# A written order for the first two recurrence blocks and their weights

## The chip, the cores and the metric

The kernel runs on one core of a Trainium2 chip. The metric is the device time of one launch in microseconds (us). TensorE (PE) multiplies matrices, VectorE (DVE), ScalarE (ACT) and GpSimd (POOL) do elementwise work, and SyncE (SP) only issues transfers; a transfer is run by 16 DMA engines. Each engine takes its instructions in the order in which its queue holds them, and waits where an operand is not there yet.

## The reference

One decoder layer on 2048 tokens of width 1024 in float32. The first half is normalised by its root mean square, projected, and given to two groups of heads that work side by side: a state-space mixer (SSD) with a short convolution, and an RWKV-7 recurrence. Their outputs are joined, projected and added; the second half is a gated feed-forward network with a convolution of three taps. The part that this change touches is the recurrence and the projection in front of it:

```python
def step(S, inp):
    r_t, w_t, k_t, v_t, a_t, b_t = inp
    sa = jnp.einsum("bhij,bhj->bhi", S, a_t)
    S = S * w_t[:, :, None, :] + sa[..., None] * b_t[:, :, None, :] + v_t[..., None] * k_t[:, :, None, :]
    return S, jnp.einsum("bhij,bhj->bhi", S, r_t)
```

Before it, each projected column is mixed with the one of the token before (`p + (shift(p) - p) * mu`), the decay `w` comes from a small network through tanh, keys are normalised per head, and the convolution of the SSD group (four taps) works on other projected columns.

## The kernel before

The recurrence phase (`phase_R`, L640) works on blocks of 128 tokens, 16 of them. It does not step through tokens: within a block the recurrence becomes products of 64-token halves, and a triangular system that is solved by substitution. Each float32 projection is made of float16 products: rows and weights are split into a high and a low part, and three of the four products are summed.

A `Block` (L730) is a set of named lists of small steps, and each step issues one or two instructions:

- `load` (L772): rows from memory, norm, split, and two transposes by DMA (L811 high part, L804 low part) into `xt`.
- `d(g)`, g from 0 to 13 (L816): one group of 128 projected columns, 24 products `d<-xt,wr`. For the odd g follow, for a pair of groups, in block 0 a copy `raw` out of PSUM (L835), the own part on ACT (L838) and the token shift on DVE (L841); results are `WA`, `GL`, `tk`, `tr`, `tv`.
- `low` (L903) gives `WX`, `zw`, `za` (the small network for decay and gate), `scan` (L944) sums the decays to `Pi` and `Pv`, `keys` (L960) and `norm` (L967) make normalised keys, with `nq` as the only product (L973), `receptance` (L999) gives `AR`.
- `gram` (L1011): products `gr<-AR,BK` and masks to `G` on DVE (L1024).
- `solve` (L1030): `G` goes to memory (`ATd`, L1038) and back in another layout (`atl`, L1041), `xl` is a constant (L1048). Then `chain`: 31 pairs of a product (L1059) and an addition (L1065), each pair depending on the one before, all on DVE. The result goes through memory to `XT`.
- `conv(g)`, g from 0 to 7 (L849): 24 products `c<-xt,wc`, `rc` on ACT (L863), taps on POOL and DVE (L881, L887), tanh on ACT (L893), a join on DVE (L898) and a store.
- `transposed`, `values`, `own`, `turn`, `merge`, `update`, `state`, `gate`, `finish`: the second half of the recurrence. `own`, `update` and `gate` read the state by products `pq` and `zg`, and `state` makes the new one (`pS`).

The weights come in 22 loads of 512 KB (`load_w`, L705): 14 for the projection (`wr`) and 8 for the convolution (`wc`). Each load lands in a staging tile `wst`, of which the even and the odd ones have two buffers each from load 2 on, and is split by ACT (high part, L598) and DVE (low part, L599). A call of `pace` keeps loads 4 and up behind block 0's transposes in SP's queue.

What sets the order: for block 0 the list `FIRST` is written for DVE and ACT, the other engines follow the scheduler. For block 1 (`SECOND`) the scheduler orders all engines. From block 2 on all engines but PE follow the list `PLAN`, whose steps are single ones. PE's order is the scheduler's throughout this phase.

Of the kernel before, what the change touches and what calls it, by code (L numbers as in the profile page):

```python
# [228 lines left out]
FIRST = """  # L229
w.0 w.1 l. w.2 w.3 w.4 w.5 f.d.0 f.d.1 f.low.0 f.d.2 f.d.3 f.d.4 w.6 f.low.1 w.7 f.d.5 f.scan w.8 f.keys w.9 w.10  # L230
f.norm f.d.6 f.d.7 w.11 w.12 f.d.8 f.d.9 f.receptance w.13 f.gram.0 w.14 f.d.10 w.15 f.gram.1 w.16 w.17 w.18 w.19
f.solve.1 f.chain.0 f.d.11 f.conv.0 f.chain.1 n.load f.conv.1.0 f.chain.2 f.taps.1 f.conv.2 f.d.12 f.chain.3 w.20
f.conv.3.0 f.transposed.0 w.21 f.conv.4 f.chain.4 f.chain.5 f.transposed.1 f.d.13 f.taps.3 f.conv.5.0 f.conv.6
f.chain.6 f.taps.5 f.chain.7 f.conv.7.0 f.taps.7
"""
# [404 lines left out]
def phase_R(tc, K, const, tables, x, w_r, w_c, wl_d, g2_d, XN, XC, YR, iters=16):  # L640
    nc = tc.nc
    V, S, G_ = nc.vector, nc.scalar, nc.gpsimd
    with ExitStack() as ctx:
# [86 lines left out]
        class Block(Steps):  # L730
# [1977 lines left out]
```

## Time and profile before

| what | value |
|---|---|
| median of the runs | 2508.16 us (2506.9 to 2513.34) |
| the profiled execution | 2506.49 us |
| its span | 2504.7 us |
| PE busy | 2396.9 us, 96% of the span |
| DVE / ACT / POOL busy | 1911.8 / 1197.9 / 1079.8 us |
| first product of PE | 15.5 us after the span's start |
| chain of block 0 begins | 68.6 us |
| chain of block 1 begins | 138.8 us |

How to read it: one execution is profiled, and its own time lies 1.8 us over its span. A row of the list in order of time has the start, the duration, the engine, the line, the operation with its output and inputs, and, in brackets, how long the engine had been idle and what released it. A `q` behind an engine (SPq) marks the issuing of a transfer. Where equal rows stand one behind another, one row covers several and gives their count.

### The profile page before, as it was taken

The numbers are of one execution on the slowest core, as the hardware profiler recorded it, in microseconds if no ns is written. First come the engines' busy times: TensorE is split into PE (matmuls) and PEld (weight loads), VectorE is DVE, ScalarE is ACT, GpSimd is POOL, SyncE is SP. The second block draws the span as 40 slices with busy tenths as digits, with TensorE's granted clock in tenths as the row PEclk, the third lists the DMA queues.
The fourth block names the chain that finished last, engine by engine and source line by source line (L and its number), as shares of the span: only waits on it lengthen the run. The fifth ranks groups of instructions, "written<-read, shape, count | busy, mean of one in ns | idle before, by whom it ended". The sixth has DMA issues, their size and how long they took to land. (4 is left out here: it accounts for less than half of the span.)

```text
span 2504.7 us, 53819 instructions
## 1 busy us (share of the span) xinstructions
PE 2396.9 (96%) x21212; PEld 1519.2 (61%) x21212; DVE 1911.8 (76%) x3790; ACT 1197.9 (48%) x2407; POOL 1079.8 (43%) x1134
## 2 busy tenths in 40 slices
PE   4899999999999999999988999999989999999998
PEld 4789999999999755555533444444434444444443
DVE  6767877787778667677999799999999735546557
ACT  6555666566656554445555544453543432213132
POOL 2243444344434532223335658685847522213135
PEclk8899999999999999999999999999999999999999
DMA  7233233323332536565774544444446533333243
GB/s 223 69 72 73 57 74 77 75 57 68 81 76 59 158 118 174 162 174 163 198 230 159 180 154 141 167 151 171 141 162 196 171 101 101 105 102 97 89 160 109
DMA packets 344412, 319.12 MB, mean 127 GB/s; under 512 B 203232, under 2 KB 248672, under 8 KB 340832
## 3 DMA queue, kind: packets, MB, share of 16 engines
q1 hardware_dynamic: 344016, 315.43, 43.1%
q8 instruction: 166, 2.72, 0.4%
q14 instruction: 86, 0.70, 0.1%
q10 hardware_dynamic: 144, 0.26, 0.0%
HBM read 187.85 MB, written 110.99 MB: 119 GB/s over the span
## 5 line engine op out<-in xcount | busy, mean ns | idle before, releaser
L2142 PE MATMUL u<-b,w 128*128 128x512 f16 x3696 | 808.5, 381 | 24.5 <-ACT C L2160 11.5
L2142 PEld LDWEIGHTS <-w 128*128 128x128 f16 x3696 | 362.8, 98 | 466.7 <-issue 35.6
L635 PE MATMUL d<-xt,wr 128*128 128x129 f16 x5376 | 335.6, 225 | 19.3 <-DMA xt<-xh 15.5
L635 PEld LDWEIGHTS <-wr 128*128 128x128 f16 x5376 | 322.0, 100 | 33.2 <-ACT wr L598 15.5
L2382 PE MATMUL d<-dw,fa 128*128 128x512 f16 x1512 | 333.6, 380 | 4.0 <-DMA dw<-DW 2.2
L2382 PEld LDWEIGHTS <-fa 128*128 128x128 f16 x1596 | 157.1, 98 | 204.7 <-issue 18.3
L2164 DVE TENSOR_TENSOR C<-u,C 128x512 f32<-128x512 f32 x220 | 150.5, 684 | 157.1 <-PE u L2142 151.4
L635 PE MATMUL c<-xt,wc 128*128 128x131 f16 x3072 | 197.9, 225 | 9.6 <-ACT rc L863 3.5
L635 PEld LDWEIGHTS <-wc 128*128 128x128 f16 x3072 | 183.8, 99 | 16.6 <-issue 9.3
L2395 DVE TENSOR_TENSOR acc<-d,acc 128x512 f32<-128x512 f32 x212 | 140.0, 682 | 54.3 <-PE d L2382 53.4
L1993 POOL TENSOR_TENSOR fa<-p,fa 128x512 f16<-128x512 f32 x100 | 140.7, 1421 | 50.7 <-ACT fa L1988 50.7
L2199 DVE SCALAR_TENSOR_TENSOR p<-C,fpar,p 128x1024 f32<-128x1024 f32 x88 | 124.3, 1412 | 34.5 <-ACT p L2195 34.4
L1995 DVE SCALAR_TENSOR_TENSOR w<-us,w 128x512 f16<-128x512 f32 x132 | 133.1, 1020 | 7.0 <-ACT w L1988 5.9
L887 DVE SCALAR_TENSOR_TENSOR ca<-c,cw,ca 128x128 f32<-128x128 f32 x360 | 113.5, 344 | 25.6 <-ACT ca L877 21.2
L1059 DVE TENSOR_TENSOR tmp<-atl,xl 128x60 f32<-128x60 f32 (+24 forms) x465 | 118.4, 255 | 16.4 <-DMA atl<-ATd 4.8
L2160 ACT ACTIVATE C<-u 128x512 f32<-128x512 f32 x88 | 52.2, 593 | 158.1 <-PE u L2142 134.4
L2199 DVE SCALAR_TENSOR_TENSOR a<-C,fpar,a 128x1024 f32<-128x1024 f32 x88 | 124.9, 1419 | 3.8 <-ACT a L2195 2.5
L1988 ACT ACTIVATE fa<-p 128x512 f16<-128x512 f32 x110 | 65.4, 623 | 124.6 <-DVE p L2212 112.7
L1065 DVE TENSOR_TENSOR xl<-xl,tmp 128x60 f32<-128x60 f32 (+24 forms) x465 | 112.5, 242 | 14.4
L1988 ACT ACTIVATE w<-us 128x512 f16<-128x512 f32 x132 | 80.2, 624 | 85.0 <-POOL us L2115 29.1
L2205 POOL COPY fcarry<-C 128x2 f32<-128x2 f32 x88 | 37.4, 426 | 161.2 <-DVE C L2164 161.2
L2115 POOL TENSOR_TENSOR us<-us,us 128x512 f32<-128x512 f32 x51 | 83.9, 1648 | 45.8 <-DVE w L1995 27.3
(334 smaller groups left out, 4308.1 us busy)
## 6 DMA issues: line engine op xcount, KB each, us to landing
UW<-w SPq DMA_DIRECT2D x154, 256.0 KB
w<-UW SPq DMA_DIRECT2D x154, 256.0 KB
us<-in_w_u_dram SPq DMA_DIRECT2D x88, 256.0 KB
DW<-dw SPq DMA_DIRECT2D x70, 256.0 KB
dw<-DW SPq DMA_DIRECT2D x56, 256.0 KB
hs<-HN SPq DMA_DIRECT2D x48, 256.0 KB
r<-in_w_d_dram SPq DMA_DIRECT2D x10, 1024.0 KB
xin<-in_x_dram SPq DMA_DIRECT2D x16, 512.0 KB
```

What stands on the lines that cost most here:

```text
L635: nc.tensor.matmul(ps, w[:, a, kt, :], xt[:, b, kt, cols], start=n == 0, stop=n == 3 * KT - 1)
L887: V.scalar_tensor_tensor(out=acc[:, q], in0=m["rc", e][:, q, k:k + 128], scalar=cw[:, e + q, k:k + 1], in1=acc[:, q], op0=ALU.mult, op1=AL ...
L1059: chain.tensor_tensor(out=self.tmp[:, :k, :n], in0=self.atl[:, j, j + 1:32].unsqueeze(1).to_broadcast([P, k, n]), in1=self.xl[:, :k, j:j + ...
L1065: chain.tensor_tensor(out=self.xl[:, :k, j + 1:32], in0=self.xl[:, :k, j + 1:32], in1=self.tmp[:, :k, :n], op=ALU.add)
L1988: S.activation(h, src, AF.Copy, **({} if scale is None else {"scale": scale}))
L1993: {"V": V, "G": G_}[engine].tensor_tensor(out=l, in0=src, in1=h, op=ALU.subtract)
L1995: V.scalar_tensor_tensor(out=l, in0=src, scalar=scale, in1=h, op0=ALU.mult, op1=ALU.subtract)
L2142: nc.tensor.matmul(bk[at], self.w[i][:, u, k, :], self.half.b[i][:, k, v, :], start=start and n == 0, stop=n == 11, skip_group_check=True)
L2164: op("V", .61, lambda: V.tensor_tensor(out=part(j, x), in0=bk[at], in1=part(*a), op=ALU.add), (("u", 4 * s + at), (*(c0, c1)[a[0]], a[1])) ...
L2199: V.scalar_tensor_tensor(out=o[j], in0=C[j][:, 2 - d:1026 - d], scalar=cw(g, 2 - d), in1=o[j], op0=ALU.mult, op1=ALU.add)
L2382: nc.tensor.matmul(bk[s, t], pairs[m].a[i][:, u, t * P:t * P + P], pairs[m].w[n][0][:, v, :], start=new and m == 0 and u == v == 0, stop=m ...
L2395: V.tensor_tensor(out=acc[j][:, t], in0=bk[s, t], in1=acc[j][:, t], op=ALU.add)
```

## The change

`FIRST`, `SECOND`, `load_w`, `load_wl`, the rule that paces the loads and the change of hands between blocks are replaced by one list, `HEAD`, of 665 single steps of blocks 0 and 1 and of the loads, followed by ACT, DVE, POOL and SP from the start. Loads and splits become steps too (`L.w.n/0` is the load n, the steps behind are its high and low parts, `L.low` is the two tiles of `wl`). PLAN is run from block 2. The instructions are the same, and so are the tiles and the arithmetic; only their order on the engines differs, up to the place where block 2 begins. The list ends with all of block 1's `solve`, so that the steps of it that PLAN's first round had issued are not issued again there.

```diff
-FIRST = """
-w.0 w.1 l. w.2 w.3 w.4 w.5 f.d.0 f.d.1 f.low.0 f.d.2 f.d.3 f.d.4 w.6 f.low.1 w.7 f.d.5 f.scan w.8 f.keys w.9 w.10
...
+HEAD = """
+L.w.0/0 L.low/3 R0.load/1 R0.load/2 L.w.0/5 R1.scan/2 R0.load/3 R0.load/0 L.w.1/0 L.w.2/0 R0.load/4 L.low/0 R0.load/5
...
-        def load_w(n):
...
-            d = nc.sync.dma_start(st, src[g:g + ng, :, k:k + nk, :].rearrange("g p k c -> p g k c"))
-            if n > 3:
-                pace(tc, K, d, "turned")
-            for i in range(nk):
-                split_w(tc, dst[:, g:g + ng, 0, k + i], dst[:, g:g + ng, 1, k + i], st[:, :, i], V, gwr[:, k + i:k + i + 1])
+        class Loads(Steps):
...
+            def w(self, n):
...
+                def rows():
+                    st = self.st[n] = wk.tile(
+                        [P, ng, nk, P], F32, name=f"wst{n}", tag="AR" if n < 2 else ("BT", "UV")[n % 2], bufs=2)
+                    nc.sync.dma_start(st, src[g:g + ng, :, k:k + nk, :].rearrange("g p k c -> p g k c"))
+
+                def hi(i):
+                    S.activation(dst[:, g:g + ng, 0, k + i], self.st[n][:, :, i], AF.Identity, scale=gwr[:, k + i:k + i + 1])
+
+                def lo(i):
+                    V.scalar_tensor_tensor(
+                        out=dst[:, g:g + ng, 1, k + i], in0=self.st[n][:, :, i], scalar=gwr[:, k + i:k + i + 1],
+                        in1=dst[:, g:g + ng, 0, k + i], op0=ALU.mult, op1=ALU.subtract)
+
+                return [rows, *(f for i in range(nk) for f in (lambda i=i: hi(i), lambda i=i: lo(i)))]
...
-        held = ExitStack()
-        held.enter_context(tc.manual_schedule(engines={getattr(mybir.EngineType, x) for x in ("DVE", "Activation")}))
-        for it in range(iters - 1):
...
+        loads = Loads()
+        K.hand.enter_context(tc.manual_schedule(engines=HANDS))
+        for step in HEAD.split():
...
+        for it in range(2, iters - 1):
+            for step in PLAN.split():
```

Below, names carry the block first (`tmp_0`, `tmp_1`), then a number of the buffer; lines of the changed kernel lie 54 to 81 higher than those of the old one.

At the start of the program, the queue of SP. Before:

```order
L663 DMA wls1_278<-in_wl_dram 128x512
L713 DMA wst2_282<-in_w_r_dram 128x4x256
L713 DMA wst3_288<-in_w_r_dram 128x4x256
L1048 DMA xl_0_800<-in_cst_dram 128x256
L811 DMA_TRANSPOSE xt_0_237<-xh_0_239 128x8x128
L804 DMA_TRANSPOSE xt_0_237<-xin_0_190 128x8x128
L713 DMA wst4_294<-in_w_r_dram 128x4x256
L713 DMA wst5_300<-in_w_r_dram 128x4x256
```

Now:

```order
L788 DMA wst2_263<-in_w_r_dram 128x4x256
L766 DMA wls0_265<-in_wl_dram 128x512
L788 DMA wst3_269<-in_w_r_dram 128x4x256
L788 DMA wst4_286<-in_w_r_dram 128x4x256
L788 DMA wst5_289<-in_w_r_dram 128x4x256
L892 DMA_TRANSPOSE xt_0_237<-xh_0_239 128x8x128
L885 DMA_TRANSPOSE xt_0_237<-xin_0_190 128x8x128
L788 DMA wst6_302<-in_w_r_dram 128x4x256
```

Loads 4 and 5 now stand ahead of the two transposes that the first product needs, and the load of `xl` stands later.

In the chain of block 0, the queue of DVE. Before, where the taps of the convolution (L887) and the splits of loads 20 and 21 (L599) stand in groups between pieces of the chain:

```order
L887 SCALAR_TENSOR_TENSOR ca_0_0_925<-rc_0_1_915,cw_216,ca_0_0_925 128x128 x6
L898 SCALAR_TENSOR_TENSOR ca_0_0_925<-ct_0_0_934,ca_0_0_925 128x256
L1059 TENSOR_TENSOR tmp_0_802<-atl_0_795,xl_0_800 128x4x19
L1065 TENSOR_TENSOR xl_0_800<-xl_0_800,tmp_0_802 128x4x19
L1059 TENSOR_TENSOR tmp_0_802<-atl_0_795,xl_0_800 128x4x18
```

Now:

```order
L1140 TENSOR_TENSOR tmp_0_981<-atl_0_888,xl_0_634 128x3x22
L794 SCALAR_TENSOR_TENSOR wc_203<-wst20_1022,gwr_235,wc_203 128x4x128
L1146 TENSOR_TENSOR xl_0_634<-xl_0_634,tmp_0_981 128x3x22
L1140 TENSOR_TENSOR tmp_0_981<-atl_0_888,xl_0_634 128x3x21
L794 SCALAR_TENSOR_TENSOR wc_203<-wst21_1045,gwr_235,wc_203 128x4x128
L1146 TENSOR_TENSOR xl_0_634<-xl_0_634,tmp_0_981 128x3x21
L1140 TENSOR_TENSOR tmp_0_981<-atl_0_888,xl_0_634 128x3x20
L968 SCALAR_TENSOR_TENSOR ca_0_0_976<-rc_0_1_968,cw_216,ca_0_0_976 128x128
```

Single splits and single taps stand between a product and its addition, or between two pairs.

At the start of block 2, the queue of DVE again. Before:

```order
L1059 TENSOR_TENSOR tmp_1_2093<-atl_1_2086,xl_1_2091 128x6x11
L841 SCALAR_TENSOR_TENSOR WA_2_2326<-d_2_0_2275,mus_204,WA_2_2326 128x128
L1065 TENSOR_TENSOR xl_1_2091<-xl_1_2091,tmp_1_2093 128x6x11
L841 SCALAR_TENSOR_TENSOR GL_2_2327<-d_2_0_2275,mus_204,GL_2_2327 128x128
L781 COPY xt_3_2397<-xt_2_2256 128x16x3
L1059 TENSOR_TENSOR tmp_1_2093<-atl_1_2086,xl_1_2091 128x6x10
L1065 TENSOR_TENSOR xl_1_2091<-xl_1_2091,tmp_1_2093 128x6x10
L914 TENSOR_TENSOR WX_2_2369<-WA_2_2326,WX_2_2369 64x128
```

Now:

```order
L1140 TENSOR_TENSOR tmp_1_2100<-atl_1_2022,xl_1_1953 128x8x2
L1314 TENSOR_TENSOR S0_0_227<-tS_01_2068,pS_01_2128 64x4x64
L1146 TENSOR_TENSOR xl_1_1953<-xl_1_1953,tmp_1_2100 128x8x2
L1140 TENSOR_TENSOR tmp_1_2100<-atl_1_2022,xl_1_1953 128x8
L1146 TENSOR_TENSOR xl_1_1953<-xl_1_1953,tmp_1_2100 128x8
L922 SCALAR_TENSOR_TENSOR WA_2_2323<-d_2_0_2272,mus_204,WA_2_2323 128x128
L922 SCALAR_TENSOR_TENSOR GL_2_2324<-d_2_0_2272,mus_204,GL_2_2324 128x128
L862 COPY xt_3_2394<-xt_2_1880 128x16x3
```

Block 2's token shift (`WA`, `GL`) was cut into the chain of block 1 two thirds of the way through, and now stands behind its last pair. PE's queue, which the scheduler sets, follows from this: `nq` of block 0 stood behind the fourth group of projections (d 4) and now stands behind d 6 and the first half of d 8; the products d 6 of block 1 now stand behind all of block 0's chain, since DVE's token shift of d 2 does.

More of the change, by code (lines that the diff above doesn't have):

```diff
@@ L228 @@
 )
-FIRST = """
-w.0 w.1 l. w.2 w.3 w.4 w.5 f.d.0 f.d.1 f.low.0 f.d.2 f.d.3 f.d.4 w.6 f.low.1 w.7 f.d.5 f.scan w.8 f.keys w.9 w.10
[L231 to L234, printed above, removed]
@@ new lines @@
+R0.receptance/3 L.w.16/1 R0.gram.0/2 R0.gram.1/2 L.w.17/1 R0.solve.1/1 R0.solve.1/0 L.w.17/3 L.w.16/3 R0.gram.1/1
+R0.d.11/1 R0.d.11/2 R1.load/5 L.w.17/4 R0.solve.1/3 L.w.16/4 L.w.18/1 R1.load/6 L.w.16/2 L.w.18/3 L.w.17/2
+R0.transposed.0/0 R0.d.12/0 R0.d.11/4 R0.solve.1/2 R0.conv.0/0 R0.d.11/3 L.w.19/1 R0.solve.1/4 L.w.19/2 L.w.18/4
+L.w.18/2 R0.conv.1.0/0 R0.conv.2/0 R0.conv.3.0/0 R1.load/7 R0.solve.1/6 R0.conv.1.0/1 R0.transposed.1/0 R0.solve.1/5
+R0.taps.1/0 L.w.19/3 R0.solve.1/7 L.w.19/4 R0.chain.0/0 R0.chain.0/1 R0.chain.0/2 R0.chain.0/3 R0.d.13/0 R0.chain.0/4
@@ new lines @@
+R1.d.5/1 R0.taps.7/6 R1.d.5/3 R0.taps.7/5 R1.d.5/2 R1.low.1/4 R0.taps.7/7 R1.low.1/2 R0.taps.7/8 R1.d.7/0 R1.low.1/3
+R1.d.5/4 R1.low.1/6 R1.keys/0 R1.d.8/0 R0.taps.5/0 R0.taps.7/9 R1.d.7/2 R2.load/1 R1.keys/1 R0.values/4 R0.chain.7/7
+R0.taps.5/1 R1.d.7/1 R1.norm/0 R1.d.7/3 R1.d.7/4 R0.taps.5/3 R0.taps.5/5 R1.norm/1 R0.taps.5/2 R0.chain.7/8 R1.scan/0
+R0.own.0/0 R1.d.9/0 R1.conv.0/0 R0.taps.5/4 R1.norm/4 R1.norm/2 R1.low.1/9 R1.scan/1 R1.d.9/1 R1.load/10 R1.low.1/7
+R0.taps.5/7 R1.low.0/6 R0.taps.7/10 R1.norm/5 R1.d.9/2 R1.norm/3 R1.conv.1/0 R0.taps.5/6 R1.d.9/3 R1.scan/3 R1.low.1/8
@@ new lines @@
+R0.taps.5/8 R1.d.9/4 R1.norm/9 R1.conv.1/1 R0.taps.5/9 R1.conv.2/0 R1.conv.1/2 R1.receptance/0 R1.conv.3/0 R0.own.0/1
+R1.conv.1/4 R1.conv.4/0 R1.conv.1/3 R1.norm/7 R1.conv.1/6 R1.norm/6 R0.chain.7/9 R1.scan/4 R0.chain.7/10 R0.chain.7/11
+R1.conv.1/5 R0.taps.5/10 R1.norm/10 R1.conv.1/7 R1.conv.1/8 R1.conv.1/9 R1.norm/8 R1.norm/11 R0.own.0/2 R0.turn/0
+R0.turn/1 R0.merge.0/0 R0.chain.7/12 R1.conv.1/10 R1.conv.3/1 R1.conv.3/3 R1.conv.3/2 R0.chain.7/13 R1.conv.3/5
+R1.norm/12 R0.merge.0/2 R1.conv.3/4 R0.merge.0/1 R1.gram.0/0 R1.gram.0/1 R1.conv.3/7 R1.gram.0/2 R2.load/2 R1.conv.3/6
@@ new lines @@
+R0.merge.1/0 R1.gram.1/0 R1.conv.5/0 R0.merge.1/1 R0.update.0/0 R1.conv.5/1 R1.gram.1/1 R1.gram.1/2 R1.conv.3/8
+R1.receptance/2 R2.load/0 R1.conv.3/9 R1.conv.6/0 R1.conv.3/10 R1.conv.1/11 R2.load/3 R1.receptance/4 R1.conv.5/2
+R1.solve/0 R1.conv.5/4 R0.update.0/1 R1.conv.5/3 R1.conv.5/5 R1.receptance/3 R1.solve/1 R1.conv.5/7 R1.solve/3
+R1.solve/2 R2.load/4 R1.conv.7/0 R1.conv.3/11 R1.solve/8 R2.load/5 R2.load/6 R0.state.0/2 R0.merge.1/2
+R1.transposed.0/0 R1.conv.7/1 R1.conv.5/6 R1.conv.5/8 R0.state.0/5 R0.own.1/0 R1.d.10/0 R1.solve/4 R0.state.0/3
@@ new lines @@
+R1.conv.7/2 R1.conv.7/4 R0.state.0/4 R1.conv.7/6 R1.receptance/1 R0.state.0/6 R1.conv.7/3 R1.solve/7 R0.own.1/1
+R2.load/7 R0.gate/0 R1.solve/5 R0.own.1/2 R0.update.1/0 R0.update.1/1 R0.state.1/5 R0.state.1/6 R0.finish.0/0
+R0.state.1/0 R0.state.1/1 R1.solve/6 R1.d.11/0 R1.conv.7/8 R1.conv.7/5 R1.conv.7/7 R1.d.11/1 R1.solve/9 R1.solve/10
+R1.solve/11 R1.conv.5/9 R1.solve/12 R1.solve/13 R1.solve/14 R1.solve/15 R1.solve/16 R1.solve/17 R1.solve/18
+R1.solve/19 R1.solve/20 R1.solve/21 R1.solve/22 R1.solve/23 R1.solve/24 R1.solve/25 R1.solve/26 R1.solve/27
@@ L241 @@
+R1.conv.5/11 R1.solve/55 R1.solve/56 R0.finish.0/4 R1.solve/57 R1.d.13/3 R1.solve/58 R1.solve/59 R1.solve/60
+R1.solve/61 R1.solve/62 R1.solve/63 R1.solve/64 R0.gate/1 R1.solve/65 R1.solve/66 R1.solve/67 R1.transposed.1/0
+R0.state.1/3 R1.solve/68 R1.solve/69 R1.solve/70 R1.solve/71 R1.solve/72 R1.solve/73 R1.conv.7/11 R1.solve/74
+R1.solve/75 R1.solve/78 R1.solve/76 R2.load/10 R1.transposed.1/1 R1.solve/77
 """
```

104 lines of the change are left out of this document (62 added, 42 removed).

## The prediction

> **What bounds the kernel now.** I read the page first, then a table of stretches over the first 200 us, then the waits of TensorE, then the order in time of the places where it waits. From the page:
>
> ```profile
> span 2504.7 us, 53819 instructions
> PE 2396.9 (96%) x21212; PEld 1519.2 (61%) x21212; DVE 1911.8 (76%) x3790; ACT 1197.9 (48%) x2407; POOL 1079.8 (43%) x1134
> PE   4899999999999999999988999999989999999998
> ```
>
> TensorE (PE) is busy for 96% of the span, and its first slices (62.6 us each) are the empty ones. The table of stretches has, for each, its length, then busy time of PE, weight loads, VectorE (DVE), ScalarE (ACT), GpSimd, then PE's granted clock, the DMA share and GB/s:
>
> ```profile
> 12.00:16.00 4.00, 0.27 (x1) 0.14 (x2) 3.94 (x8) 4.00 (x8) 0.00 (x0) 1.00 1.12 202
> 16.00:28.00 12.00, 11.79 (x159) 11.77 (x158) 8.28 (x17) 8.44 (x23) 0.14 (x1) 1.00 1.08 323
> 28.00:52.00 24.00, 9.92 (x107) 8.39 (x105) 17.14 (x27) 18.80 (x37) 9.43 (x10) 0.73 0.48 147
> 52.00:69.00 17.00, 12.95 (x150) 11.41 (x149) 13.01 (x22) 9.38 (x16) 2.68 (x3) 0.80 0.58 160
> 69.00:84.00 15.00, 9.38 (x75) 8.12 (x74) 13.59 (x46) 5.21 (x10) 4.09 (x5) 0.61 0.73 185
> 84.00:105.00 21.00, 20.94 (x318) 20.10 (x319) 15.27 (x63) 9.40 (x28) 2.46 (x5) 0.93 0.11 24
> 105.00:146.00 41.00, 37.05 (x637) 34.54 (x635) 26.79 (x82) 22.92 (x47) 13.20 (x15) 1.00 0.28 65
> 146.00:166.00 20.00, 17.78 (x270) 16.26 (x267) 15.68 (x53) 10.90 (x30) 8.27 (x8) 1.00 0.05 8
> 166.00:200.00 34.00, 34.00 (x605) 32.18 (x604) 24.89 (x82) 20.01 (x42) 13.09 (x16) 1.00 0.46 95
> ```
>
> From 166 us on PE is full; before that it idles: 15.5 us before its first product, 14.1 in 28 to 52, 4.1 in 52 to 69, 5.6 in 69 to 84, 4.0 in 105 to 146, 2.2 in 146 to 166, 46 with the crumbs. That is all this change can touch: the products stay the same, and from block 2 on each engine keeps its order. So I forecast when block 2's first projections end, and carry that shift to the end. Where the middle ones come from (engine, line, total, times, longest), for PE from 28 to 146 us:
>
> ```profile
> PE nq L973 <- ACT sq L964: 9.0, 1, 9.0
> PE gr L1019 <- DVE AR L1006: 5.1, 1, 5.1
> ```
>
> The key norm `nq` holds PE while its input is made elsewhere, and the gram waits for DVE.
>
> **The change part by part.** First the **start**. Rows are start, duration, engine, line, operation, and in brackets the idle time before and its releaser:
>
> ```profile
> 11.20 1.35 SPq L811 DMA_TRANSPOSE xt<-xh  x1
> 15.52 0.27 PE L635 MATMUL d<-xt,wr 128*128 128x129 f16 x1 [15.52 <-DMA xt<-xh]
> 21.50 0.39 ACT L835 ACTIVATE raw<-d 128x258 f32<-128x258 f32 x1
> ```
>
> The first product waits for the transpose, issued at 11.20 and done at 15.5. Now loads 4 and 5 (1.05 MB) stand ahead of it and the 0.13 MB load of `xl` does not: 0.92 MB more. At the 323 GB/s of 16 to 28 us that is 2.8 us, if the transposes wait for the bytes ahead; 0 if they overtake them. I take 2.8: the first product at 18.3, `raw` at 24.3. [...]
>
> **From `raw` to the chain of block 0.** First two stretches in the columns of the table above, from `raw` to the end of ACT's split of load 15 and (for the next part) from the chain of block 0 to block 1's d 6; then rows in order of time:
>
> ```profile
> 21.50:53.40 31.90, 17.82 (x226) 16.06 (x224) 22.80 (x41) 25.70 (x56) 9.57 (x10) 0.77 0.61 191
> 68.60:104.70 36.10, 30.25 (x391) 27.99 (x389) 29.22 (x108) 14.71 (x37) 6.25 (x10) 0.80 0.36 90
> ...
> 51.40 2.08 PE L1019 MATMUL gr<-AR,BK 64*128 64x128 f32 x16 [5.09 <-DVE AR L1006]
> 52.09 1.33 ACT L598 ACTIVATE wc<-wst,gwr 128x512 f16<-128x512 f32 x2 [1.94 <-DMA wst<-in_w_c_dram]
> 57.52 1.28 DVE L1024 TENSOR_TENSOR G<-gr,cst 128x512 f32<-128x512 f32 x2
> 58.83 0.82 SPq L1038 DMA_DIRECT2D ATd<-G  x2
> 64.42 1.71 SPq L1041 DMA_DIRECT2D atl<-ATd  x4
> 68.61 0.19 DVE L1059 TENSOR_TENSOR tmp<-atl,xl 128x31 f32<-128x31 f32 x1 [2.45 <-DMA atl<-ATd]
> ```
>
> ACT is busy for 25.70 of the 31.9 us; with the same steps packed it would be at that place at 24.3 + 25.7 = 50.0 instead of 52.09 + 1.33 = 53.4. `nq` now stands behind d 6, so PE does not wait 9.0 us for it, and the weights are split earlier. But the gram does not profit by 9: it waits for `AR` on DVE, which waits for ACT and GpSimd, and PE comes to it at 51.8 by the same walk (before 51.40). Its masks `G` end about 1 us earlier, at 57.9; with the 68.61 - 58.80 = 9.8 us that the round trip through DRAM takes, `atl` would be there at 67.7; the loads that it shared the queue with are further ahead, and DVE's own list (split of load 19) is done at 67.2. I take the latter: **-1.4** (bounds: -4.2 where the transposes overtake the loads, +1 where ACT loses 2.4 of its 3.4 again).
>
> **The chain of block 0.** The solve is 31 pairs of a product and an addition on DVE:
>
> ```profile
> L1059 DVE TENSOR_TENSOR tmp<-atl,xl 128x60 f32<-128x60 f32 (+24 forms) x465 | 118.4, 255 | 16.4 <-DMA atl<-ATd 4.8
> L1065 DVE TENSOR_TENSOR xl<-xl,tmp 128x60 f32<-128x60 f32 (+24 forms) x465 | 112.5, 242 | 14.4
> 76.65 1.66 DVE L887 SCALAR_TENSOR_TENSOR ca<-rc,cw,ca 128x128 f32<-128x128 f32 x6
> 78.79 0.42 DVE L898 SCALAR_TENSOR_TENSOR ca<-ct,ca 128x256 f32<-128x256 f32 x1 [0.48 <-ACT ct L893]
> 81.28 2.73 DVE L599 SCALAR_TENSOR_TENSOR wc<-wst,gwr,wc 128x512 f16<-128x512 f32 x4
> 103.26 5.68 PE L635 MATMUL d<-xt,wr 128*128 128x129 f16 x96
> ```
>
> The 31 pairs take 15.4. In the last row 24 products end d 4 of block 1, then d 6 begins: 103.26 + 24/96 x 5.68 = 104.7, 36.1 us after the chain began. In these DVE was busy for 29.22 us (the second stretch above) and idle for 6.9; PE was short of work in 69 to 84 and full in 84 to 105: it did late what waited for taps and splits behind pieces of the chain. The list now mixes single taps and splits into the chain, and d 6 of block 1 stands behind DVE's token shift of d 2, which stands just behind the chain's end. DVE has till there 31 x (0.255 + 0.242) = 15.4, twelve taps 12 x 0.277 = 3.3, four splits 2.7, two joins 0.8, and some 12 small steps that I price at 0.3 each, 3.7: 25.9 us if nothing makes it wait (3.3 of the 29.22 now stand before or after it). PE's own work from 60 us up to there, some 25.6 us of products, would end at 85.6, so DVE decides: d 6 at 67.2 + 25.9 = 93.1 instead of 104.7. That is **-10.2**, the largest term; its bounds are -19 (PE's floor) and -3.3 (DVE waits as long as before, 6.9).
>
> **From there to block 2.** This took from 104.7 to 145.7 (below), 37.05 of it busy, the same as in 105 to 146. The second half of `za` and the first reading of the state (`pq`) move into it:
>
> ```profile
> 100.29 1.15 PE L1179 MATMUL pq<-UV,G 64*64 64x64 f32 x32
> 102.36 0.39 PE L928 MATMUL zw<-WX,wl 128*128 128x128 f16 x4
> 102.81 0.39 PE L928 MATMUL za<-WX,wl 128*128 128x128 f16 x4
> ```
>
> `pq` takes 102.36 - 100.29 = 2.1, `za` 103.26 - 102.81 = 0.45: 39.6 of work. Of the 4.0 of stalls I keep 1.5 (the others end on DVE and ACT steps that the list puts earlier), and add 1.5 for some 15 hand-overs between engines at 0.1 that a walk by durations does not see: 42.6, **+1.6** (bounds -1.4 and +4).
>
> **Block 2's first projections.** The list finishes all of block 1's chain before DVE's token shift of block 2:
>
> ```profile
> 138.83 0.19 DVE L1059 TENSOR_TENSOR tmp<-atl,xl 128x31 f32<-128x31 f32 x1 [2.36 <-DMA atl<-ATd]
> 144.28 4.31 PE L635 MATMUL d<-xt,wr 128*128 128x129 f16 x72
> 151.96 0.34 DVE L841 SCALAR_TENSOR_TENSOR WA<-d,mus,WA 128x128 f32<-128x128 f32 x1
> 154.78 0.39 PE L928 MATMUL zw<-WX,wl 128*128 128x128 f16 x4
> 161.23 4.30 PE L635 MATMUL d<-xt,wr 128*128 128x129 f16 x72
> ```
>
> d 0 of block 2 began at 144.28 + 1.44 = 145.7; `WA` was cut into the chain at 151.96; `zw` needed it. Now the gram ends at 93.1 + 20.5 of products + 0.5, its masks at 115.3, the chain begins 9.8 later at 125 and takes 15.4 + 3.6 of other steps, so `WA` at 144 and `zw` at 145.8, 1.8 later. PE, with d 0 begun at 135.7, reaches `zw` 8.1 us later at 143.8 (before 154.78 - 145.7 = 9.1, about 1 of it waiting): a wait of 2.0 in place of the 2.2 there: **0**. Behind `WA` stand on DVE `GL`, the copy of `xt` and `WX`; ACT's tanh waits for it.
>
> **The clock.** It was 0.73 in 28 to 52 and 0.61 in 69 to 84, behind long waits. Fewer long waits mean less of that, but a walk at full speed between 42 and 70 us is too good: 0 to +2, I take **+1.0**. [...]
>
> **Sum:** -1.4 - 10.2 + 1.6 + 0 + 1.0 = -9.0 us. The profiled execution took 2506.49 (span 2504.7 and 1.8 around it), 1.7 below the median of 2508.16. I take the sum off the median: 2508.16 - 9.0 = 2499. With its bounds the forecast's own range is a gain of 3 to 15: 2493 to 2505.
>
> **Rivals.**
> **Larger gain:** the transposes overtake the loads, the chain starts at about 64, and DVE's small steps find free slots, so that PE is nearly at its floor: 2.8 + about 13, near 16 us, 2492. For it speaks that DVE was idle for 6.9 us there; against, that the chain's 15.4 us cannot shrink.
> **No change:** the start costs 2.8, ACT's packed walk slips by 3 (a step written in order makes all behind it wait), the pieces of the chain wait as before: -9.0 + 6 = a gain of about 3, 2505. For it speaks that ACT is busy for only 18.8 of 24 us in 28 to 52 although its order was written already.
> **Slower:** block 1's chain ahead of `WA`. If its `atl` arrives no earlier than in the trace (138.83), `WA` is at 157.8 and `zw` at 159.6 against 154.78: +4.8, and up to +8 with the clock halved after that wait, about 2514. It decides from a chain start of about 134 on. Against it: the gram in front stands earlier by 10 us.
> That the change does nothing is excluded: PE's queue differs from the first 48 products on.
>
> **How the numbers follow.** A measurement here tells about 0.3% from no change, 7.5 us. Forecast 0.55, of which 0.45 lies above 7.5 us; larger gain 0.20; no change 0.15; slower 0.10, of which 0.08 is beyond 7.5 us; what is left of each counts as no change. Faster 0.45 + 0.20 = 0.65, slower 0.08, the same 0.27. The range reaches from 2487 (larger gain with all bounds good: 21 us, the -19 with the better start) to 2508 (no gain): about 0.1 is left out above, less below.
>
> **What would show it.** In the changed kernel: the first product at 18.3 (15.5 if transposes overtake); no wait at `nq`; the chain of block 0 at 67.2 and d 6 of block 1 at 93.1 (the step most likely to fail); d 0 of block 2 at 135.7; a wait of about 2 at `zw`; from there the same products in the same time. I am wrong if DVE waits inside the first chain, or if d 6 comes after 100.

## The result, and the profile after

The changed kernel takes 2491.06 us (median of 5 runs, 2487.77 to 2499.62), the kernel before 2508.16 (median of 5 runs, 2505.32 to 2513.34). The ratio is 0.9934, with a 95% interval of 0.9912 to 0.9957: 17 us by the medians, 11 to 22 by the interval. The prediction was 2499 with a range of 2487 to 2508.

The profiled execution is the slowest of the five (2499.62). Its page:

```profile
span 2497.8 us, 53811 instructions
PE 2398.1 (96%) x21210; PEld 1519.3 (61%) x21212; DVE 1909.4 (76%) x3790; ACT 1197.4 (48%) x2407; POOL 1082.4 (43%) x1134
```

The busy times over the whole span are those of before. The table of stretches of the changed kernel, in the same cuts and columns as before:

```profile
16.00:28.00 12.00, 6.74 (x84) 6.30 (x85) 8.18 (x15) 6.81 (x16) 0.00 (x0) 1.00 0.90 249
28.00:52.00 24.00, 16.34 (x209) 15.08 (x206) 18.96 (x33) 22.31 (x49) 10.26 (x10) 0.79 0.55 178
52.00:69.00 17.00, 12.00 (x161) 11.34 (x160) 14.97 (x25) 9.20 (x17) 6.83 (x6) 0.89 0.77 193
69.00:84.00 15.00, 13.25 (x201) 12.53 (x198) 14.33 (x62) 6.24 (x16) 1.10 (x2) 1.00 0.20 49
84.00:105.00 21.00, 20.87 (x352) 19.87 (x350) 18.80 (x60) 14.62 (x34) 9.03 (x12) 1.00 0.37 91
105.00:146.00 41.00, 39.54 (x673) 37.15 (x672) 31.33 (x115) 22.03 (x53) 13.75 (x14) 1.00 0.28 54
146.00:166.00 20.00, 20.00 (x362) 18.41 (x361) 13.71 (x33) 14.52 (x30) 10.79 (x13) 1.00 0.34 85
```

In 16 to 28 us PE is worse off (6.74 busy instead of 11.79) and in 52 to 69 no better (12.00 instead of 12.95). In the others it is better off or as good: 16.34 instead of 9.92 in 28 to 52, 13.25 instead of 9.38 in 69 to 84, and full in 146 to 166, where it had lost 2.2. The waits of PE up to 170 us (total, times, longest; four of them) show that the long waits at `nq` and for `AR` are gone and shorter ones stand elsewhere instead:

```profile
PE d L689 <- ACT wr L791: 17.9, 1, 17.9
PE d L689 <- ACT tr L919: 4.8, 1, 4.8
PE c L689 <- ACT tv L919: 3.5, 1, 3.5
PE nq L1054 <- ACT sq L1045: 1.0, 1, 1.0
```

The places in time on which the prediction stood, in the changed kernel (start, duration, operation): the first product, the products with both parts of the rows, the first and the last pair of block 0's chain, d 6 of block 1, the first pair of block 1's chain, d 0 and `WA` of block 2, and the key norm `nq` of block 2.

```profile
17.91 0.27 PE L689 MATMUL d<-xt,wr 128*128 128x129 f16 x1 [17.91 <-ACT wr L791]
18.61 5.58 PE L689 MATMUL d<-xt,wr 128*128 128x129 f16 x70 [0.43 <-DMA xt<-xin]
68.25 0.18 DVE L1140 TENSOR_TENSOR tmp<-atl,xl 128x31 f32<-128x31 f32 x1
88.53 0.18 DVE L1140 TENSOR_TENSOR tmp<-atl,xl 128x8 f32<-128x8 f32 x1
90.30 1.55 PE L689 MATMUL d<-xt,wr 128*128 128x129 f16 x24
119.67 0.18 DVE L1140 TENSOR_TENSOR tmp<-atl,xl 128x31 f32<-128x31 f32 x1
131.27 2.93 PE L689 MATMUL d<-xt,wr 128*128 128x129 f16 x48
137.21 0.34 DVE L922 SCALAR_TENSOR_TENSOR WA<-d,mus,WA 128x128 f32<-128x128 f32 x1
148.33 1.12 PE L1054 MATMUL nq<-sq,cst 128*128 128x512 f32 x2
```

The last of these before:

```profile
165.37 1.08 PE L973 MATMUL nq<-sq,cst 128*128 128x512 f32 x2
```

So the key norm of block 2 comes 165.37 - 148.33 = 17.0 us earlier, the gain of the medians. The term that made most of it lies between the start of block 0's chain and d 6 of block 1: 90.30 - 68.25 = 22.05 us, before 36.1.

The 17.0 us can also be split by what PE did. The first 166 us, before and now:

```profile
0.00:166.00 166.00, 120.06 (x1702) 110.73 (x1702) 117.35 (x329) 96.12 (x203) 44.73 (x60) 0.90 0.45 124
0.00:166.00 166.00, 128.75 (x2020) 120.67 (x2022) 125.79 (x359) 105.91 (x226) 56.23 (x70) 0.96 0.49 132
```

PE idled 45.9 us before and idles 37.3 now, 8.7 less. The other 8.3 us are products that take less time: up to the key norm of block 2 PE is busy for 111.1 us now (128.75 less the full stretch from 148.33 to 166) and was busy for 119.4, with 1700 products in both traces. The granted clock is the third figure from the right: its mean over these 166 us is 0.96 instead of 0.90.

**One thing must be taken out of the profiled span.** It is only 2504.7 - 2497.8 = 6.9 us shorter. The other 10 us were lost after 800 us, where nothing was changed, at the passage from the recurrence to the next phase. There PE waits as long as before (3.1 us, before 3.2), and the granted clock falls earlier and for longer (its mean is 0.91 over the 130 us from 813 on, before 0.97 over the 130 us from 830 on). First the wait, the stretch behind it and a later stretch before, then the same of the changed kernel:

```profile
PE vt L1112 <- ACT tg L1255: 3.2, 1, 3.2
850.00:860.00 10.00, 9.94 (x136) 7.68 (x135) 5.91 (x14) 5.27 (x12) 8.07 (x20) 1.00 0.11 25
880.00:890.00 10.00, 9.37 (x102) 5.80 (x104) 4.80 (x7) 4.68 (x12) 1.15 (x2) 0.66 0.59 187
```

```profile
PE vt L1193 <- ACT tg L1336: 3.1, 1, 3.1
833.50:843.50 10.00, 10.00 (x104) 7.60 (x103) 3.03 (x9) 4.42 (x10) 6.97 (x19) 0.66 0.02 9
873.50:883.50 10.00, 10.00 (x62) 5.19 (x62) 4.64 (x8) 3.15 (x9) 2.68 (x3) 0.50 0.43 158
```

The granted clock stayed at 1.00 behind the wait before and fell to 0.66 here; later it fell in both, to 0.66 before and to 0.50 here. For that reason the experiments are read by the key norm of block 2 and not by one span.

### The profile page after: what moved, and what is told of

It is laid out like the page before. It is cut to its first block, busy times and chain, and to the rows that moved or that the text cites. A ratio compares the mean times of both kernels' runs of the same rounds, so it can differ in the third digit from the quotient of the medians.

```text
span 2497.8 us, 53811 instructions
## 1 busy us (share of the span) xinstructions
PE 2398.1 (96%) x21210; PEld 1519.3 (61%) x21212; DVE 1909.4 (76%) x3790; ACT 1197.4 (48%) x2407; POOL 1082.4 (43%) x1134
## 5 line engine op out<-in xcount | busy, mean ns | idle before, releaser
L2051 ACT ACTIVATE w<-us 128x512 f16<-128x512 f32 x132 | 80.3, 624 | 85.6 <-PE u L2205 28.6
```

The costliest lines, as they stand in the source:

```text
L2051: S.activation(h, src, AF.Copy, **({} if scale is None else {"scale": scale}))
```

## The experiments

All start from the changed kernel but one, which starts from the one before. Times in us; the third column is d 6 of block 1, the fourth the key norm of block 2; the rest is the span less the fourth.

| kernel | chain of block 0 | d 6 | key norm | span | rest |
|---|---|---|---|---|---|
| before | 68.6 | 104.7 | 165.4 | 2504.7 | 2339.3 |
| changed | 68.3 | 90.3 | 148.3 | 2497.8 | 2349.5 |
| changed, again | 66.8 | 88.8 | 146.9 | 2490.1 | 2343.2 |
| loads 4 and 5 swapped | 68.0 | 90.1 | 148.0 | 2497.2 | 2349.2 |
| load steps by the list | 65.7 | 87.7 | 145.7 | 2487.9 | 2342.2 |
| tv early | 66.8 | 89.2 | 147.3 | 2488.6 | 2341.3 |
| split early | 66.8 | 90.3 | 148.3 | 2491.1 | 2342.8 |
| chain in closed pieces | 68.4 | 96.2 | 154.2 | 2494.6 | 2340.4 |
| block 1's chain left to the steady list | 67.1 | 89.1 | 146.8 | 2490.1 | 2343.3 |
| first part written only | 68.4 | 91.0 | 156.6 | 2498.0 | 2341.4 |
| second part written only | 76.4 | 96.5 | 154.5 | 2495.1 | 2340.6 |
| before, key norm late | 70.7 | 107.4 | 168.0 | 2512.0 | 2344.0 |
| three edits together | 65.8 | 88.3 | 146.3 | 2489.3 | 2343.0 |
| and tr early | 67.1 | 91.0 | 150.3 | 2488.7 | 2338.4 |

**The changed kernel again**, no edit.

> The changed kernel once more, unchanged. Its first profile gained 17.0 us up to the key norm of block 2 (165.37 before, 148.33 after), but only 6.9 in the span, because TensorE's clock fell to 0.66 and 0.50 in two stretches of 10 us between 833 and 884 us behind a wait of 3.1 us, which in the kernel before (3.2 us) left the clock at 1.00. Theory A (the clock drop is a matter of one execution): the key norm of block 2 is at 148.3 +-0.3 again, and the span is either near 2488 without the drop or near 2498 with it. Theory B (the drop belongs to the changed kernel): the clock is below 0.7 at the same place again and the span is 2497 to 2499.

The key norm came at 146.85, outside the 0.3 that I had allowed, since the chain started 1.4 us earlier: the head differed by about 1.5 us between the two executions. The clock fell again (0.66 in 830 to 840, 0.78 and 0.70 in 860 to 880), but less, and the span is 2490.1. Neither theory holds as put: the drop is not always the same, and it is not a matter of one execution either. The rest differs from 2338 to 2350 between kernels that are the same there, and the span of one execution can't tell less than that.

**Transposes ahead of loads 4 and 5.**

```diff
- ... R0.load/8 R0.load/9 ... L.w.4/0 ... L.w.5/0 ...
+ ... R0.load/8 R0.load/9 L.w.5/0 L.w.4/0 ...
```

> Loads 4 and 5 are issued behind the two transposes instead of ahead of them, the rest of the list is unchanged. Theory A (the transposes wait for the bytes ahead of them, and the head up to the first chain is a chain of dependent steps): the first product moves from 17.9 to about 15.5 us, and block 0's solve (68.25) and the key norm of block 2 (148.3) come 2.4 us earlier. Theory B (the start is covered, because ACT and the later loads set the pace): the first product comes earlier, but block 0's solve and block 2's key norm move by less than 0.5 us. Theory C (the transposes overtake the loads): the first product stays at 17.9, which its row puts down to ACT's split.

This moved nothing but the order of loads 4 and 5 between themselves. The list names the transposes ahead of both loads already, but block 0's `load` is called in full before the list begins, so its places in the list are empty, and SP had both loads first. The run is one more execution of the changed kernel as far as the rest goes: 148.0.

**Block 0's load steps by the list.**

```diff
         blocks = [Block(it) for it in range(iters)]
-        blocks[0].do("load")
         loads = Loads()
```

> The earlier try to put the transposes ahead of loads 4 and 5 only swapped those two loads, because block 0's load steps are issued before the list begins, so their places in the list do nothing. Here that call in front is taken out, and the load steps follow the list: both transposes stand ahead of loads 4 and 5 in SP's queue, and ACT splits one piece of a weight before the norm. Theory A (bytes issued ahead delay the transposes): the transposes are issued at about 10.6 us as before, the first product comes at 15.5 to 16.5 instead of 17.9. What follows of it: if the head is one chain of dependent steps, the start of block 0's solve (68.25, 66.8 and 68.0 in three looks) and the key norm of block 2 (148.3, 146.9, 148.0) come 2 us earlier; if ACT and the later loads set the pace, both stay in 66.5 to 68.5 and 146.5 to 148.5; since loads 4 and 5 now wait for the transposes to be issued, they could even be 1 to 2 us later. Theory B (transposes overtake, ACT's split sets the start): the first product stays at 17.7 to 18.4.

From the list in order of time:

```profile
14.07 0.27 PE L689 MATMUL d<-xt,wr 128*128 128x129 f16 x1 [14.07 <-DMA xt<-xh]
14.92 5.18 PE L689 MATMUL d<-xt,wr 128*128 128x129 f16 x61 [0.58 <-DMA xt<-xin]
```

With both parts PE begins at 14.92 instead of 18.61: 3.7 us earlier, of which 0.5 is from an earlier issue of the transposes (10.12 instead of 10.61). From the issue of the first transpose to this product it takes 8.0 us in the changed kernel and in the run with loads 4 and 5 swapped, where the two loads stand ahead, and 4.8 here, where they do not. So here the transposes waited for the bytes ahead of them; the 2.8 us of the prediction were 3.2. But behind that the chain starts only 1.1 to 2.6 us earlier than in the three executions of the unchanged order, and so does all else: PE waits for ACT's own parts of `tr` (6.1 us) and `tk` (2.3) and for splits on DVE (2.4) in between. About half of what the start loses is covered later.

**One step of ACT earlier, two ways.** `tv` is what PE waits for before the first convolution product (3.5 us); the split is what DVE waits for ahead of the chain (1.9 us).

```diff
- R0.d.11/1 R0.d.11/2 R1.load/5 ... R1.load/6 ... R0.d.11/3 L.w.19/1
+ R0.d.11/1 R0.d.11/2 R0.d.11/3 R1.load/5 ... R1.load/6 ... L.w.19/1
```

> One ACT step is moved: the second half of the own part of group 11 (tv) directly behind its first half, ahead of block 1's norm, its float16 copy and two splits. In the changed kernel PE waits 3.46 us for it before the first convolution product (61.8). Theory P (in the chain's time PE is full from there to d 6 of block 1, so an earlier convolution carries through): the first convolution product moves 2.5 to 3 us ahead, d 6 of block 1 from 22.0 us to 20 us or less behind the chain's start or the chain starts earlier too, and the key norm of block 2 comes at 144.5 to 146. Theory D (DVE's list decides when d 6 starts): the convolution starts earlier, but d 6 and the key norm of block 2 stay (146.5 to 148.5), because the chain does not start earlier.

```diff
- R0.conv.1.0/1 ... L.w.19/3 R0.solve.1/7 L.w.19/4 R0.chain.0/0
+ L.w.19/3 R0.conv.1.0/1 ... R0.solve.1/7 L.w.19/4 R0.chain.0/0
```

> One ACT step is moved: the last high part of load 19 ahead of the copy of the first convolution group out of PSUM, for which ACT waited 4.0 us; DVE's low part of it stands directly ahead of the chain and waited 1.9 us. Theory D (DVE's list decides): the chain starts about 2 us earlier (at 65.5 to 66.5), and d 6 of block 1 and the key norm of block 2 come 2 us earlier (145 to 146.5). Theory P (PE is full): the chain starts earlier, d 6 comes no more than 0.5 us earlier, and the key norm of block 2 stays at 146.5 to 148.5.

With `tv` early (the first convolution products and the next ones):

```profile
57.38 0.98 PE L689 MATMUL c<-xt,wc 128*128 128x131 f16 x14
61.88 3.08 PE L689 MATMUL c<-xt,wc 128*128 128x131 f16 x34 [3.52 <-DVE wc L794]
```

The convolution begins 3.3 to 4.4 us earlier, and d 6 (89.2) and the key norm (147.3) lie where theory D has them. But the run does not decide against theory P: after 14 products PE waits 3.5 us for a split on DVE, and the second pair of convolution groups begins at 65.44, just as in the second execution of the changed kernel. The convolution as a whole was not earlier. With the split early (start of the chain, a split in it, its last pair, d 6):

```profile
66.75 0.18 DVE L1140 TENSOR_TENSOR tmp<-atl,xl 128x31 f32<-128x31 f32 x1
72.97 0.75 DVE L794 SCALAR_TENSOR_TENSOR wc<-wst,gwr,wc 128x512 f16<-128x512 f32 x1 [1.24 <-ACT wc L791]
88.49 0.17 DVE L1140 TENSOR_TENSOR tmp<-atl,xl 128x8 f32<-128x8 f32 x1
90.25 1.55 PE L689 MATMUL d<-xt,wr 128*128 128x129 f16 x24
```

The chain begins earlier for its head and ends no earlier: from its first to its last pair it takes 21.7 us instead of 20.3. Most of this is the 1.24 us that a split in it waits for ACT; on ACT the split stood, in order, behind a copy out of PSUM, for which PE had the convolution group at 70.10, 3.0 us after ACT's copy of the group before (done at 67.09). By its numbers that is theory P, though the row shows another reason than a full PE. In both executions of the changed kernel and in these two, d 6 starts 1.75 to 1.77 us behind the last pair of the chain, as soon as DVE's token shift of d 2 has ended (at 90.24 in the changed kernel, where d 6 starts at 90.30), so DVE releases it; but what stands in the chain needs the convolution, so an earlier chain alone waits. And PE is there hardly earlier than DVE. The last products ahead of d 6 in the changed kernel:

```profile
89.78 0.39 PE L1013 MATMUL zw<-WX,wl 128*128 128x128 f16 x4
```

d 6 follows 0.52 us behind this start. In the closed pieces and the two halves below, where d 6 is not held, it follows 0.22 to 0.26 us behind. So DVE's list and PE's own products come to this place within 0.3 us of each other.

**The chain in closed pieces.** The pairs stand together, 12, 12 and 7, and behind each piece what stood between its pairs.

```diff
- ... R0.chain.0/3 R0.d.13/0 R0.chain.0/4 R0.taps.1/1 R0.taps.1/2 R0.conv.3.0/1 R0.chain.0/5 ...
+ ... R0.chain.0/3 R0.chain.0/4 R0.chain.0/5 ...
...
+ R0.chain.2/7 R0.d.13/0 R0.taps.1/1 R0.taps.1/2 R0.conv.3.0/1 ...
```

> Block 0's 31 pairs stand in DVE's queue in three closed pieces (12, 12 and 7 pairs); the taps, splits and token shifts that stood between single pairs now stand behind the piece. Theory A (the gain of 14 us between the start of the chain and d 6 of block 1 comes from mixing single steps in, because PE waits for those steps): d 6 of block 1 moves from 90.3 to 96 or later, the key norm of block 2 from 148.3 to 154 or later. Theory B (what counts is that DVE's sum of steps is short and never waits; the mixing is unimportant): both move by less than 1 us.

```profile
75.03 0.39 ACT L944 ACTIVATE rc<-c 128x262 f32<-128x262 f32 x1 [7.51 <-DVE tv L922]
75.47 2.45 PE L689 MATMUL d<-xt,wr 128*128 128x129 f16 x24 [3.28 <-ACT rc L944]
90.83 0.17 DVE L1140 TENSOR_TENSOR tmp<-atl,xl 128x8 f32<-128x8 f32 x1
96.17 1.55 PE L689 MATMUL d<-xt,wr 128*128 128x129 f16 x24
```

Theory A: d 6 moves from 90.3 to 96.2, the key norm to 154.2. The rows show the way it goes: `tv` on DVE now stands behind 12 pairs; ACT, in order, waits 7.5 us for it before it can copy a convolution group out of PSUM; PE waits 3.3 us for that copy. The chain itself takes 22.5 us instead of 20.3 from its first to its last pair, and d 6 follows 5.3 us behind the last pair instead of 1.8. Against these closed pieces the mixing is worth 5.9 us of the 14; the other 8 no run takes apart.

**Block 1's chain left to the steady list.** The steps from `R1.solve/35` on are taken out of `HEAD`; PLAN's first round then issues them, between the steps of block 2.

```diff
- R1.solve/35 R1.solve/36 R1.solve/37 R1.solve/38 R1.solve/39 R0.finish.0/1 ...
+ R0.finish.0/1 ...
```

> The pairs of block 1's solve from the 14th on, and the transfers behind them, are left to the steady list, which cuts block 2's token shift into the chain as the kernel before did. Theory A (block 1's chain is early enough, so its place ahead of the token shift costs nothing): the key norm of block 2 stays at 148.3 within 0.5 us, the one of block 3 at 198.6 within 0.5 us. Theory B (finishing the chain first is part of the gain): block 2's second half waits for the solve and the key norm of block 3 comes 1 us or more later. Theory C (the rival of the prediction: the chain ahead of the token shift costs time): the key norm of block 2 comes earlier by 1 us or more.

The key norms of blocks 2 and 3 come at 146.8 and 196.9, in the second execution of the changed kernel without an edit at 146.9 and 197.1. The times that theory A names are missed by 1.5 us, and 146.8 against 148.3 would even be theory C; but that is the head, which differs as much between two executions of the same kernel. From d 6 of block 1 to the key norm of block 2 it takes 57.7 us, in the two executions of the changed kernel 58.0. So theory A: where block 1's chain stands costs 0.3 us at most.

**Half of the list.** In the first of these the scheduler orders the engines from the end of block 0's chain to block 2, in the second up to that end (there the written order is entered at this step, not left).

```diff
         for step in HEAD.split():
+            if step == "R0.transposed.1/1":
+                held.close()
...
```

> The written order holds up to the end of block 0's chain; from there to block 2 the scheduler orders all engines again, from the same list of steps. Theory A (the gain is earned in block 0's chain): d 6 of block 1 stays near 90 and from there to the key norm of block 2 it takes 58 us, as in the changed kernel, or at most 3 more, 60.7 in the kernel before; so the key norm of block 2 is at 147 to 151. Theory B (block 1's order matters as much): the key norm of block 2 is at 155 or later.

> The other half: the scheduler orders everything up to the end of block 0's chain, and the written order holds from there. Theory A (the gain is earned in block 0's chain): d 6 of block 1 comes at 100 or later, as in the kernel before (104.7), and the key norm of block 2 at 158 or later. Theory B (block 1's order earns it): the key norm of block 2 is at 153 or earlier.

With the first part written, d 6 comes at 91.0, but from there to the key norm it takes 65.6 us (changed 58.0, before 60.7). With the second part written, the gram waits 8.5 us for DVE and the chain begins 8 us late (the second row):

```profile
61.60 2.50 PE L1100 MATMUL gr<-AR,BK 64*128 64x128 f32 x18 [8.47 <-DVE BK L1075]
76.36 0.19 DVE L1140 TENSOR_TENSOR tmp<-atl,xl 128x31 f32<-128x31 f32 x1 [8.27 <-DMA atl<-ATd]
```

And yet d 6 comes 20.2 us behind it, even less than the 22.0 of the changed kernel. In the first run theory B holds (156.6), in the second neither does (96.5 and 154.5): the gain is not earned in one half. Written order up to the end of block 0's chain is worth some 6 us here (154.5 against 148.3) and written order behind it some 8 (156.6), each from one execution, and each measured against the scheduler's order of this list, which is not that of the kernel before. That d 6 follows in 20 us there too fits DVE's queue in that kernel, where the scheduler too puts one or two taps between the pairs of the chain (the splits were done before it).

**The kernel before with its key norm late.**

```diff
- f.keys w.9 w.10 f.norm f.d.6 f.d.7 w.11
+ f.keys w.9 w.10 f.d.6 f.d.7 f.norm w.11
```

> The kernel before with one word of its list moved: block 0's norm behind d 6 and d 7, so that PE does not wait 9.0 us for the key norm with products at hand. Theory A (the step of the prediction: that wait is not worth its length, since ACT and the loads set when the gram and the chain come): PE's wait there shrinks to below 2 us, but block 0's solve starts within 1.5 us of 68.6 and the key norm of block 2 within 1.5 us of 165.4. Theory B (the wait is on the path): both come 5 us or more earlier. Theory C: the norm's later steps on DVE and ACT come later, and the solve starts 2 us or more later.

```profile
PE gr L1019 <- DVE AR L1006: 8.8, 1, 8.8
PE d L635 <- ACT wr L598: 6.4, 2, 4.9
70.73 0.19 DVE L1059 TENSOR_TENSOR tmp<-atl,xl 128x31 f32<-128x31 f32 x1 [2.94 <-DMA atl<-ATd]
```

The wait of 9.0 us at `nq` is gone, 6.4 us of waiting for splits stand in front instead, the gram waits 8.8 instead of 5.1, and the chain starts 2.1 us later: theory C. Taking out a wait of 9.0 us of the engine that bounds the kernel won nothing in this way. But the edit also moves the norm's own steps back (`nq` comes at 41.62 instead of 37.16), it is one execution, and 2.1 us is not far above the 1.5 by which heads of the same program differ; what the wait would be worth with the norm in its old place was not tested.

**The three edits together, and a fourth.** The fourth puts ACT's `raw` and `tr` of d 6 ahead of six splits (`R0.d.7/1` to `/3` ahead of `L.w.13/1`).

> Three edits together: block 0's load steps follow the list, the second half of tv stands behind its first half, and ACT's last high part of load 19 stands ahead of the copy of the first convolution group. Alone, the first brought the key norm of block 2 to 145.7, and each of the other two left it (147.3 and 148.3, against 146.9 to 148.3 unchanged). Theory A (chain and convolution bind together, so that each edit alone meets the other bound): the chain starts 2 us earlier than with the first edit alone (65.7), at 63 to 64, runs its 20.3 us without waiting, d 6 of block 1 starts at 85 to 86 (87.7), the key norm of block 2 at 143 to 144, and the time is 3 us or more below the changed kernel's 2491. Theory B (something else, PE or a load, binds just behind): the chain starts earlier but lasts 22 us or more, and the key norm of block 2 stays at 145 to 146.

```profile
65.79 0.21 DVE L1140 TENSOR_TENSOR tmp<-atl,xl 128x31 f32<-128x31 f32 x1 [1.24 <-DMA atl<-ATd]
```

The chain starts no earlier than with the first edit alone (65.79 against 65.69), takes 20.8 us to its last pair, and the key norm is at 146.3, so theory A falls. Of theory B the reason holds but not the numbers: something else binds just behind the other two, here the round trip of the solve's matrix through memory, for which the chain now waits 1.2 us. The head of this execution was also 1 us later from the first product on (14.93 against 14.07). The time is 2489.14 us (median of 6), ratio 0.9927 (0.9912 to 0.9942) to the kernel before; against the changed kernel's 0.9934 (0.9912 to 0.9957) that is no difference that these runs show.

> The three edits of the run before, and with them ACT's copy and own part of group 7 (raw and tr of d 6) ahead of six weight splits. PE waits 6.1 us for it before d 10 with the first edit alone. Theory A (ACT has to do all of these splits before d 10 can end, so the wait moves and does not shrink): d 10 starts earlier, PE waits for a split instead, and the gram, the chain and the key norm of block 2 stay within 0.7 us of the run before. Theory B (the wait is on the path): the gram and all behind it come 2 us or more earlier.

Its median lies 6.4 us above that of the run before it: 2495.57 us (median of 5), ratio 0.9957 (0.9942 to 0.9972), an interval that just touches the other; the key norm is at 150.3. PE's wait for `tr` did not shrink (6.5 us), and a wait of 2.3 us for a split came on top. So neither theory holds. That the edit makes ACT's splits later fits, but ACT also waited 2.0 us longer for a load ahead of the edit in that one execution, and how much is the edit's was not separated.

## Why the prediction was right, and where its terms were not

The direction, the range and the step that carries most of the gain were right. The point, 2499, was 8 us too high: the forecast's own range (2493 to 2505) ends 2 us above the time, and the time is that of the rival with the larger gain (2492). The stated range holds it because it reached down to that rival. Term by term:

- **The start and block 0's head, -1.4.** The first product came at 17.91, where I had put it at 18.3, and its row is released by a split on ACT; the products with both parts, which wait for the transposes, came at 18.61 against 16.21 in the kernel before. The transposes waited for the bytes ahead of them, as taken. The run with the load steps by the list has 3.2 us for the two loads (8.0 us from the issue to the products with both parts, 4.8 without the loads ahead), where the estimate from the bytes and 323 GB/s was 2.8. The chain began at 68.25 instead of 67.2, at 66.8 to 68.0 in the other executions, 68.6 before: -0.4 in the profiled execution. The step that "the gram does not profit by 9" from the wait at `nq` was right: the wait is 1.0 us now, and the gram comes at 53.28 where it came at 51.40. The bound that held the chain was not DVE's own list, as I had it, but the wait of the split ahead of it for ACT, which stood behind PE (its copy of the first convolution group waited 4.0 us for it):

```profile
67.45 0.88 DVE L794 SCALAR_TENSOR_TENSOR wc<-wst,gwr,wc 128x512 f16<-128x512 f32 x1 [1.92 <-ACT wc L791]
```

- **The chain of block 0, -10.2.** The mechanism was right (DVE's list releases d 6) and its size was off: 22.05 us instead of 25.9, so -14.0. The term that was mis-sized is the price of the steps between the pairs. PE's floor was mis-sized too: it was to be done at 85.6, but the convolution began only at 61.82 and waited twice more, and PE came to d 6 at about 90.0, 0.3 us ahead of DVE, so a shorter list alone would have gained 0.3 us at most there. Rows of the changed kernel, first where steps stand in the chain, then from block 1's chain, where none do:

```profile
73.68 0.22 DVE L1140 TENSOR_TENSOR tmp<-atl,xl 128x69 f32<-128x69 f32 x1
73.82 0.35 DVE L968 SCALAR_TENSOR_TENSOR ca<-rc,cw,ca 128x128 f32<-128x128 f32 x1
74.08 0.23 DVE L1146 TENSOR_TENSOR xl<-xl,tmp 128x69 f32<-128x69 f32 x1
74.34 0.23 DVE L1140 TENSOR_TENSOR tmp<-atl,xl 128x66 f32<-128x66 f32 x1
74.49 0.75 DVE L794 SCALAR_TENSOR_TENSOR wc<-wst,gwr,wc 128x512 f16<-128x512 f32 x1
75.15 0.22 DVE L1146 TENSOR_TENSOR xl<-xl,tmp 128x66 f32<-128x66 f32 x1
```

```profile
123.42 0.23 DVE L1140 TENSOR_TENSOR tmp<-atl,xl 128x69 f32<-128x69 f32 x1
123.69 0.23 DVE L1146 TENSOR_TENSOR xl<-xl,tmp 128x69 f32<-128x69 f32 x1
```

  A product and its addition alone start 0.27 apart; with a tap between them 0.40, with a split 0.81. So a tap costs 0.13 there, not the 0.277 that it takes in a row of its kind, and a split 0.54, not 0.68: about 0.14 less each. With 25 steps between the pairs (12 taps, 4 splits, a join, 8 small ones) that is 3.5 us, an estimate that takes the 0.14 of taps and splits for all of them; four more steps stand behind the last pair, one small step fewer in all than I had priced at 0.3. 25.9 - 3.5 - 0.3 = 22.1.
- **From d 6 to block 2, +1.6.** It took 131.27 - 90.30 = 40.97, as before (41.0): -0.1. In this stretch PE was busy for 39.5 us and idle for 1.5, so the work (39.6) and the stalls (1.5) were as worked out; the 1.5 us for hand-overs did not come on top. The 0.1 us for each of them was my estimate, and no run shows it as a term: the waits that the profile of the changed kernel lists for PE in this stretch are two of 0.7 us, both for ACT.
- **Block 2's first projections, 0.** The wait of 2.0 us at `zw` did not come, since the chain began at 119.67 and not at 125: the masks ended at 111.3 and not at 115.3 (2.8 of it from d 6), and the way from there to the chain was 8.4 us and not 9.8. PE is full there, 17.1 us from d 0 to the key norm instead of 19.65: -2.6. The rival that was to end slower was to decide from a chain start of 134 on, and was 14 us off; leaving the chain to the steady list changed 0.3 us at most.
- **The clock, +1.0.** The clock is better than before in these stretches (0.79 against 0.73, 0.89 against 0.80, 1.00 against 0.61), and its cost is inside the terms above; as a term of its own it was counted twice. No run shows the +1.0. The halved clock that the slower rival reckons with stands in the trace of before as 0.50 in 36 to 42 us, around the end of the wait of 9.0 us at `nq` (37.16); around `zw` of block 2, where that rival had it, no wait came and the clock was 1.00 (137 to 145 us). The premise that PE's 46 us of idling are "all this change can touch", since the products stay the same, does not hold either: 8.3 of the 17.0 us are the same number of products taking less time.

In sum: -0.4 - 14.0 - 0.1 - 2.6 = -17.1, measured -17.0; these are distances between the places above, so they must add up, and the sum is no test. Against the forecast of -9.0, what I gave away is about 3.8 us in the prices of the steps in the chain, 2.6 in the wait at `zw`, and 2.5 in two corrections that no row carried (hand-overs and clock); the start was 1.0 worse.

The rival with the larger gain had the time, but not the way: the transposes did not overtake, and the chain did not start at 64. Its last part is what happened: the small steps cost less in the chain than in a row, and PE is within 0.3 us of its own walk. What spoke for it was weaker than its number: of the 6.9 us that DVE idled there before, 3.6 lie behind 101.1, where DVE had done its last step ahead of d 6.

## What to carry to other kernels

A long chain of dependent steps on one engine was the place to put single independent steps: here they cost less between two dependent ones than in a group (0.13 us against 0.28 for a tap, 0.54 against 0.68 for a split, on DVE), and what waited for them on other engines got them early; the closed pieces cost 6 us. A wait of the bounding engine need not be worth its length: taking out one of 9.0 us by doing the norm later won nothing in the kernel before, and in the changed one each of two steps done earlier met the next bound. When TensorE's granted clock differs between two traces, compare its busy time for the same products too and not only its idling (here 119.4 and 111.1 us for 1700 products). When the change is in the first 6% of a kernel, compare the place where the changed part ends and not spans alone, and make sure that a list's entries issue what they name: eleven of these did nothing.

## What the runs showed of the hardware that was not expected

- An independent step of DVE between two dependent ones cost about 0.14 us less here than among its own kind (0.13 instead of 0.28 for a tap of 0.35, 0.54 instead of 0.68 for a split of 0.75).
- The same wait of PE at the same place did not always cost the clock, and its length did not decide. At the passage behind 800 us PE waits for `tg` for 3.2 us in the kernel before, and the granted clock behind it stayed at 1.00; it waits for 3.1 us in the changed kernel, and the clock fell to 0.66 in the next 10 us. In the second execution of the changed kernel PE is idle for 1.9 us of 820 to 840 us, and the clock is 0.66 in 830 to 840; with block 1's chain left to the steady list it is idle for 2.1 us of the same 20, and the clock stays at 1.00 up to 860. The run with loads 4 and 5 swapped (2.5 us idle there) has 0.66, the one with closed pieces (2.4 us) 1.00. The changed kernel's profiled execution, whose clock fell again to 0.50 in 873.5 to 883.5, took 10.2 us longer behind block 2's key norm than the kernel before. What decides was not shown.
- The head of the same program differed by 1.5 us between executions (chain start 66.8 to 68.3). What makes the difference is open.
